# A conditioned two-layer decoder trunk: the residual gates formed as columns on VectorE and spread through DRAM, their PSUM bank given to the transposes

## The chip, the cores and the metric

The kernel runs on one core of one Trainium2 chip. The metric is the device time of one execution in microseconds (us); lower is better. The core's engines are called PE (TensorE: matmuls and transposes), DVE (VectorE), ACT (ScalarE), POOL (GpSimd) and SP (SyncE, which here issues most DMAs). SBUF is the on-chip memory of 128 partitions; PSUM is the memory of eight banks into which PE writes.

## The reference

A sequence of 256 tokens of width 1024 passes two layers. Each layer has three sub-layers: a half-step SwiGLU feed-forward part (FFN, inner width 2816), a token mixer (MoBA attention in layer 0, MLA attention in layer 1, 16 heads each), and a second FFN. All arithmetic is float32. Every sub-layer normalizes its input, shifts and scales it, and adds its result through a gate; shift, scale and gate are vectors of 1024 that a condition vector c gives through one large matrix:

```
c_act = silu(c)
for layer in range(DEPTH):
    mods = c_act @ ada_w[layer] + ada_b[layer]
    sh1, sc1, g1, sh2, sc2, g2, sh3, sc3, g3 = jnp.split(mods, 9, axis=-1)
    h = modulate(rms_norm(x, norm_g[layer, 0]), sh1, sc1)
    x = x + 0.5 * g1[:, None, :] * swiglu(h, ...)
    h = modulate(rms_norm(x, norm_g[layer, 1]), sh2, sc2)
    x = x + g2[:, None, :] * mix
    h = modulate(rms_norm(x, norm_g[layer, 2]), sh3, sc3)
    x = x + 0.5 * g3[:, None, :] * swiglu(h, ...)
```

Layer 1 computes one more pair of shift and scale for its shared keys and values. So there are twenty vectors of 1024: six gates, and fourteen shifts and scales. Each costs a product of c_act with a 1024 x 1024 block of ada_w.

## The kernel before, in words

**Tiles and matmuls.** The 256 tokens lie in two tiles of 128 partitions (t = 0, 1). Each float32 operand of a matmul is split into a high part (hi, gh, h) and a rest (lo, gl), and a product is three matmuls (`mm3`, lines 810 to 812): hi x hi, lo x hi, hi x lo. In the FFN's first half two of the three are merged into one matmul of 512 columns (line 1015), the third has 256 (line 1023). `wload` takes the next weight tile of up to 1 MB from a stream on SP into one of three `raw` buffers (line 787), and `split` (lines 677 to 682) makes hi on ACT (line 680) and lo on DVE (line 681) into a ring of eight each.

**The stages**, with the times of the profile: the first FFN, whose first six blocks `first` computes while the first weights arrive (to about 50 us) and whose rest runs to some 213 us; MoBA to 330; the FFNs of both layers' ends and starts to 700; MLA to 800; the last FFN to the end. During the first FFN a side program builds the bias tables of MoBA. Between two stages stands a norm: `resid` (lines 916 to 931) multiplies the sum by the gate (`ry`, line 920, DVE), adds it to x (line 921) and takes the sum of squares (lines 839 to 842); `rstd_of` (line 847) raises it to the power -0.5 on POOL; ACT scales x to y (line 855), PE transposes it (line 860), ACT or DVE shifts and scales it (lines 876, 878), and the result is split into h (lines 825, 826). In the attentions `head_rstd` (line 1187) has a power on POOL for each group of heads (`hr`).

**The conditioning vectors.** `first` forms the first shift and scale itself; `ada_stream` goes through the other eighteen vectors in eight steps each, paced by PE's work (`ada_pace`). Every step loads one [128, 1024] block of 512 KB (`adaw`, line 707, SP, ring of three).
- Shifts and scales (`column`, line 688): the blocks are transposed on the host. DVE multiplies a block by c_act, which stands in all partitions (`c_b`), and sums along the row; the sum is one column of [128, 8] (line 691: the product and a short read of the accumulator).
- Gates (`ada_gate`, line 721): the blocks are not transposed. POOL clears a [128, 1024] tile `acc` (line 727) and loads the bias into its first row (line 728); DVE adds, eight times, a block times a column of c_act (line 729). Then the column sums of `acc` are wanted in all partitions: `acc` is split into hi and lo, PE multiplies each half by a matrix of ones (lines 739 and 740: four matmuls of 512 columns a gate) into the one bank of the pool `ps_ada`, and ACT copies the bank to the gate's tile with the factor 0.5 or 1 (line 742).

**PSUM.** Eight banks: four for sums (`ps_mm`), three for transposes and scores (`ps_tr`), one for the gates (`ps_ada`, line 588). `first` borrows the gates' bank for its second transpose (line 1624).

**The order.** The program's instructions are put in order by the class `Order`: it lists all with their dependences and buffers, works out when each is due, and places them one by one on the five queues with a table of costs. Then it tries changed due times: each number in `TRIALS` (line 200) is the seed of one random change, and a change is kept where the placed program comes out shorter by those costs. The order found is fixed by dependences, so each engine runs its list in just that order, and a waiting instruction holds up all that stand behind it on its engine.

Of the kernel before, what the change touches and what calls it, by code (L numbers as in the profile page):

```python
# [12 lines left out]
F32 = mybir.dt.float32  # L13
# [9 lines left out]
P = 128  # L23
# [107 lines left out]
def lay_out(v):  # L131

    import numpy as np

    def tiled(w, kt):
        return w.reshape(kt, P, -1).transpose(1, 0, 2).reshape(-1)

    out = {"w": np.concatenate([  # L140
        tiled(np.concatenate([v[n][at][k0 * P:(k0 + kt) * P, c:c + cols] for n, at, c in parts], axis=1), kt)
        for parts, k0, kt, cols in weight_tiles()])}
    out["first"] = np.stack([v["ffn_w_" + n][0, 0, :, :B1 * P].reshape(KD, P, B1, P) for n in ("gate", "up")], axis=3)
    first = out["first"].reshape(KD, P, -1)
    out["first"] = np.concatenate([first[:, :, :FIRST_A].reshape(KD, -1), first[:, :, FIRST_A:].reshape(KD, -1)], axis=1)
    mats, cols, rows = [], np.zeros((P, 3, NK), np.float32), []
    for key, i in vectors():
        w, b, c = ((v["kv_ada_w"], v["kv_ada_b"], i) if key == "kv" else
                   (v["ada_w"][key[0]], v["ada_b"][key[0]], 3 * key[1] + i))
        w, b = w[:, c * D:(c + 1) * D], b[c * D:(c + 1) * D]  # L150
        mats.append((w if i == 2 else w.T).reshape(KD, P, D))
        if i == 2:
            rows.append(b)
        else:
            c0 = NORMS.index(key) * KD
            cols[:, i, c0:c0 + KD] = b.reshape(KD, P).T
    gains = np.concatenate([v["norm_g"].reshape(6 * KD, P), v["kv_norm_g"].reshape(KD, P)])
    cols[:, 2] = gains.T
    pos = np.ascontiguousarray(v["positions"].reshape(S))
    out["c"] = np.concatenate([v["c"].reshape(4, S), np.zeros((28, S), np.float32)])  # L160
    more = [v["c"].reshape(KD, P).T, pos.view(np.float32).reshape(NT, P).T]
    for n in ("moba_q_g", "moba_k_g"):
        more.append(np.tile(v[n][0], 2)[:, None])
    for g in (v["mla_q_g"][0], v["mla_k_g"]):
        more += [np.concatenate([g[:DH], np.ones(P - DH, np.float32)])[:, None], np.tile(g[None, DH:], (P, 1))]
    out.update(ada=np.stack(mats), rows=np.stack(rows), cols=np.concatenate([cols.reshape(P, -1), *more], axis=1))


    table = np.concatenate([np.zeros((1, H), np.float32), v["rel_bias"]])
    keys = pos.view(np.float32).reshape(NT, NB, 4).transpose(0, 2, 1)[:, :, None].repeat(NB, axis=2).reshape(NT, P, NB)  # L170
    end = np.concatenate([table[-1:], np.zeros((NB - 1, H), np.float32)])
    out["tab"] = np.concatenate([*[np.tile(x, (4, 1)) for x in (table[1:], table[:-1], end)], *keys], axis=1)
    for n in ("x", "positions", "kv_a_norm_g", "mla_q_a_norm_g"):
        out[n] = v[n]
    return out


def bcast_row(ap, n, parts=P):
# [18 lines left out]
GATE_MARGIN = 3000.0  # L197
ROUND_OF_ORDER = 4

TRIALS = (23, 24, 58, 84, 106, 187, 193, 252, 302, 317, 381, 394, 424, 459, 553, 591, 607, 655, 706, 722, 891,  # L200
          1035, 1303, 1712, 2361, 2399, 2425, 2605, 2752, 3000, 3292)
ENGINES = ("PE", "DVE", "Activation", "Pool", "SP")


# [370 lines left out]
def trunk(ctx: ExitStack, tc: tile.TileContext, a: dict, out: bass.AP):  # L575
# [8 lines left out]
    sp = ctx.enter_context(tc.tile_pool(name="sp", bufs=8))  # L584
    dp = ctx.enter_context(tc.tile_pool(name="dp", bufs=1, space=DRAM))
    ps_mm = ctx.enter_context(tc.tile_pool(name="ps_mm", bufs=4, space=PSUM))
    ps_tr = ctx.enter_context(tc.tile_pool(name="ps_tr", bufs=3, space=PSUM))
    ps_ada = ctx.enter_context(tc.tile_pool(name="ps_ada", bufs=1, space=PSUM))

    uid = [0]  # L590

    def nm(s):
        uid[0] += 1
        return f"{s}_{uid[0]}"
# [23 lines left out]
    def pe(us):  # L618
        clock[0] += us
        if busy[0]:  # L620
            return
        while pend and pend[0][0] <= clock[0]:
            run_next()
        while pace[0] and clock[0] >= pace[1]:
            pace[1] += pace[0]
            ada(1)
# [23 lines left out]

    ident = cp.tile([P, P], F32, name="ident")
    make_identity(nc, ident)
    ones_r = cp.tile([P, P], F32R, name="ones_r")
    ones = ones_r.bitcast(F32)
    nc.vector.memset(ones, 1.0)
    ident_b = cp.tile([P, P], BF16, name="ident_b")
    nc.vector.tensor_copy(ident_b, ident)
    mhalf = cp.tile([P, 8], F32, name="mhalf")
# [3 lines left out]

    pos_f = a["positions"].rearrange("o s -> (o s)")

    all_cols = cp.tile([P, 3 * NK + KD + NT + 4 + 2 * RO], F32, name="cols")
    places = {}
    c0 = 3 * NK
    for name, n in (("c", KD), ("pos", NT), ("moba_q", 1), ("moba_k", 1), ("q", 1), ("q_pe", RO), ("k", 1), ("k_pe", RO)):
        places[name] = all_cols[:, c0:c0 + n]
        c0 += n  # L670
    cols, cact = all_cols[:, :3 * NK].rearrange("p (i c) -> p i c", i=3), places["c"]
# [16 lines left out]
    def column(key, i, k, wt):  # L688

        c = NORMS.index(key) * KD + k  # L690
        nc.vector.tensor_tensor_reduce(wt, wt, c_b, 1.0, cols[:, i, c:c + 1], op0=ALU.mult, op1=ALU.add,  # L691
                                       accum_out=m_cols[:, i, c:c + 1])

    def scale_col(key, k0=0, n=KD):
        s = col_slice(1, key, k0, n)
# [9 lines left out]
    def ada_tile(j, k):  # L705
        wt = adap.tile([P, D], F32, tag="adaw", name=nm("adaw"))
        nc.sync.dma_start(wt, a["ada"][j, k])
        return wt
# [11 lines left out]

    def ada_gate(j, key, row):

        for k in range(KD):
            with noted(late if key == (1, 2) else set()):
                if k == 0:
                    acc = adap.tile([P, D], F32, tag="acc", name=nm("acc"), bufs=1)
                    nc.gpsimd.memset(acc, 0.0)
                    nc.gpsimd.dma_start(acc[0:1, :], a["rows"][row:row + 1, :])
                nc.vector.scalar_tensor_tensor(acc, ada_tile(j, k), cact[:, k:k + 1], acc, op0=ALU.mult, op1=ALU.add)  # L729
            if k < KD - 1:  # L730
                yield
        ahi, alo = split(acc, D)
        t = mods[key, "g"] = modp.tile([P, D], F32, tag="gate", name=nm("gate"))

        def sums():
            for hh in range(2):
                pt = ps_ada.tile([P, 512], F32, tag="ada", name=nm("adaps"))
                sl = slice(hh * 512, (hh + 1) * 512)
                nc.tensor.matmul(pt, ones_r, ahi[:, sl], start=True, stop=False)
                nc.tensor.matmul(pt, ones_r, alo[:, sl], start=False, stop=True)  # L740
                pe(0.44)
                nc.scalar.activation(t[:, sl], pt, AF.Copy, scale=1.0 if key[1] == 1 else 0.5)
            ready.add((key, "g"))
        later(3.0, sums)
        yield

    def ada_stream():
# [440 lines left out]
        return r  # L1188


    bias_d = dp.tile([3, P // NB, P, H * NB], F32, name="bias_d")


# [371 lines left out]
    def first(units):  # L1565
# [5 lines left out]
        with ExitStack() as st:  # L1571
# [49 lines left out]
                for i in range(2):  # L1621
                    nc.scalar.activation(c_b[:, i * 512:(i + 1) * 512], pc[i], AF.Copy)
            hold(lambda: nc.scalar.activation(cact, cact, AF.Silu), 10e3)
            ps_x = [tr_tile(), ps_ada.tile([P, 512], F32, tag="ada", name=nm("tr"))]
            accs = [tr_tile() if f >= 4 else mm_tile() for f in range(B1)]


# [117 lines left out]
```

## Time and profile before

| | before |
|---|---|
| three timed runs, us | 990.71, 990.8, 993.58 |
| median, us | 990.8 |
| span of the profiled execution, first to last instruction, us | 988.2 |
| median less that span, us | 2.6 |
| TensorE clock granted, mean | 1.000 |

The profiled execution's own time is not recorded beside its span; where a span is carried over to a time, the 2.6 us of the last difference are added. The profile is of one execution. "Busy" counts the time in which an engine executes; matmul records overlap one another, so the cost of a matmul is read from the distance between starts, not from the length of a record. A row of a group gives line, engine, operation, tiles written and read, shapes and count, then busy time in us and the mean of one in ns, then the idle time just before and what ended it. A row of the timeline gives the start, the length, the engine and the line, with the idle time and its releaser in brackets.

### The profile page before, as it was taken

The page shows a single profiled execution, that of the slowest core. Times are in us where ns is not written, and L with a number is a line of the kernel's source. Part 1 is how long each engine was busy: PE and PEld are TensorE (multiplying, and loading weights), DVE is VectorE, ACT ScalarE, POOL GpSimd, SP SyncE. Part 2 cuts the span into 40 slices and gives each one's busy share as a digit, 9 for nine tenths or more (in the row PEclk, how much of TensorE's full clock was granted, in tenths as well). Part 3 has the DMA queues.
Part 4 walks back from the last instruction along what each step waited for, and adds up shares of the span by engine and source line. Part 5 has one row for each costly group of instructions (what it writes and reads, how often), then busy time and mean ns, then how long its engine had stood idle before and what let it go on. Part 6 is the DMA issues. An engine that isn't in the chain of part 4 may idle for free.

```text
span 988.2 us, 15338 instructions
## 1 busy us (share of the span) xinstructions
PE 975.4 (99%) x5580; PEld 832.0 (84%) x5583; DVE 845.5 (86%) x1433; ACT 630.4 (64%) x1180; POOL 82.7 (8%) x120
## 2 busy tenths in 40 slices
PE   8999999999999999999999999999999999999998
PEld 6988888888887788888888888888888888888887
DVE  7999999899998899999889999984899789767642
ACT  6699565378756866656367566553889796657421
POOL 1021010022230100000000000000042110000000
PEclk9999999999999999999999999999999999999999
DMA  9978989898786688888988888883343467544630
GB/s 363 409 262 289 323 305 346 321 344 305 274 322 221 228 289 326 308 299 316 353 325 308 320 325 327 297 320 108 106 158 129 171 229 265 213 188 170 233 130 22
DMA packets 53420, 260.57 MB, mean 264 GB/s; under 512 B 6208, under 2 KB 7008, under 8 KB 35168
## 3 DMA queue, kind: packets, MB, share of 16 engines
q1 hardware_dynamic: 51840, 255.93, 70.7%
q0 software_dynamic: 1024, 3.17, 1.1%
q8 instruction: 44, 0.72, 0.3%
q10 hardware_dynamic: 480, 0.49, 0.2%
q14 instruction: 32, 0.26, 0.1%
HBM read 255.37 MB, written 4.19 MB: 263 GB/s over the span
## 4 chain that ended last, share of the span: by engine, by line
PE 87%; DMA 4%; DVE 4%; issue 2%; ACT 1%; POOL 1%; SPq 0%; ACTq 0%; DVEq 0%; POOLq 0%
PE mm L1015 23%; PE mm L810 15%; PE mm L811 15%; PE mm L812 15%; PE mm L1023 12%; DMA raw<-in_first_dram 3%; PE at L1150 1%; PE at L1090 1%; PE at L1130 1%; DMA bias_d<-bt 1%; DVE lo L681 1%; PE tr L860 1%; DMA raw<-in_w_dram 1%; PE tr L1522 1%; PE at L1095 1%
## 5 line engine op out<-in xcount | busy, mean ns | idle before, releaser
L681 DVE TENSOR_TENSOR lo<-raw,hi 128x1024 fp32r<-128x1024 f32 (+3 forms) x312 | 367.8, 1197 | 69.6 <-ACT hi L680 56.3
L680 ACT ACTIVATE hi<-raw 128x1024 fp32r<-128x1024 f32 (+3 forms) x312 | 316.6, 1037 | 138.9 <-PE mm L812 100.4
L1015 PE MATMUL mm<-h,hi 128*128 128x512 f32 x1120 | 278.9, 392 | 1.0 <-DVE g L955 1.0
L1015 PEld LDWEIGHTS mm<-h,hi 128*128 128x128 f32 x1120 | 202.9, 188 | 38.6 <-DVE g L955 1.4
L1023 PE MATMUL mm<-h,lo 128*128 128x256 f32 x1120 | 157.8, 283 | 0.0
L1023 PEld LDWEIGHTS mm<-h,lo 128*128 128x128 f32 x1120 | 150.4, 191 | 8.8
L691 DVE CUSTOM_DVE_ANT_0 adaw<-adaw,c_b,cols 128x1024 f32<-128x1024 f32 x112 | 141.9, 1278 | 6.6 <-DMA adaw<-in_ada_dram 4.6
L810 PE MATMUL mm<-hi,gh 128*128 128x512 f32 (+1 forms) x356 | 138.0, 388 | 0.0
L811 PE MATMUL mm<-lo,gh 128*128 128x512 f32 (+1 forms) x356 | 137.9, 387 | 0.0
L812 PE MATMUL mm<-hi,gl 128*128 128x512 f32 (+1 forms) x356 | 137.8, 387 | 0.0
L810 PE MATMUL mm<-hi,h 128*128 128x512 f32 (+1 forms) x240 | 93.7, 398 | 0.4 <-ACT h L825 0.4
L811 PE MATMUL mm<-lo,h 128*128 128x512 f32 (+1 forms) x240 | 93.2, 392 | 0.2 <-DVE lo L681 0.2
L812 PE MATMUL mm<-hi,h 128*128 128x512 f32 (+1 forms) x240 | 91.4, 391 | 0.0
L812 PEld LDWEIGHTS mm<-hi,gl 128*128 128x128 f32 x356 | 66.9, 188 | 13.5
L811 PEld LDWEIGHTS mm<-lo,gh 128*128 128x128 f32 x356 | 66.9, 188 | 13.4
L810 PEld LDWEIGHTS mm<-hi,gh 128*128 128x128 f32 x356 | 66.9, 188 | 13.3
L729 DVE SCALAR_TENSOR_TENSOR acc<-adaw,cols,acc 128x1024 f32<-128x1024 f32 x48 | 61.8, 1287 | 0.1
L954 ACT ACTIVATE g<-mm 128x256 f32<-128x256 f32 x70 | 26.4, 377 | 54.8 <-PE mm L1023 51.6
L810 PEld LDWEIGHTS mm<-hi,h 128*128 128x128 f32 x240 | 44.9, 188 | 10.1 <-issue 1.3
L812 PEld LDWEIGHTS mm<-hi,h 128*128 128x128 f32 x240 | 45.0, 188 | 9.0 <-DVE h L826 0.4
L811 PEld LDWEIGHTS mm<-lo,h 128*128 128x128 f32 x240 | 45.1, 188 | 8.4 <-DVE lo L681 0.4
L825 ACT ACTIVATE gh<-g 128x256 fp32r<-128x256 f32 x76 | 31.1, 412 | 30.2 <-DVE g L958 30.1
(241 smaller groups left out, 1224.5 us busy)
## 6 DMA issues: line engine op xcount, KB each, us to landing
raw<-in_w_dram SPq DMA_DIRECT2D x142, 1024.0 KB, 5.5
adaw<-in_ada_dram SPq DMA_DIRECT2D x160, 512.0 KB, 5.5
raw<-in_w_dram SPq DMA_DIRECT2D x12, 512.0 KB, 3.8
raw<-in_first_dram SPq DMA_DIRECT2D x7, 512.0 KB, 9.1
raw<-in_w_dram SPq DMA_DIRECT2D x6, 576.0 KB, 3.8
bias_d<-bt SPq DMA_DIRECT2D x12, 256.0 KB, 4.9
bg<-bias_d POOLq DMA_DIRECT2D x4, 768.0 KB, 6.0
raw<-in_first_dram SPq DMA_DIRECT2D x10, 256.0 KB, 8.4
```

The costliest lines, as they stand in the source:

```text
L680: nc.scalar.activation(hi, src, AF.Copy)
L681: nc.vector.tensor_tensor(lo, src, hi.bitcast(F32), op=ALU.subtract)
L691: nc.vector.tensor_tensor_reduce(wt, wt, c_b, 1.0, cols[:, i, c:c + 1], op0=ALU.mult, op1=ALU.add, accum_out=m_cols[:, i, c:c + 1])
L729: nc.vector.scalar_tensor_tensor(acc, ada_tile(j, k), cact[:, k:k + 1], acc, op0=ALU.mult, op1=ALU.add)
L810: nc.tensor.matmul(ps, lh, rh, start=start, stop=False)
L811: nc.tensor.matmul(ps, lh, rl, start=False, stop=False)
L812: nc.tensor.matmul(ps, ll, rh, start=False, stop=stop)
L825: nc.scalar.activation(hi, ps, AF.Copy)
L860: nc.tensor.transpose(kslice(pt, j), kslice(y, j), ident)
L954: nc.scalar.activation(x, ps[:, S:], AF.Copy)
L1015: nc.tensor.matmul(ps[i], w[0], hs[2], start=k == 0, stop=False)
L1023: nc.tensor.matmul(*low[:3], start=False, stop=low[3])
```

## The change

The six gates are now formed as the shifts and scales are. The host transposes their blocks, with the rows dealt out so that the eight sums of a gate, [128, 8], hold element 8p + k in partition p and column k; their biases come in as 48 more columns of the tile `cols`, which grows from 246 to 294 columns. `column`'s instruction becomes a helper, `dot` (line 692 of the changed kernel), and `ada_gate` calls it eight times with the bias column as the start and as the place of the sum. DVE halves the sums of the four FFN gates (line 730), a POOL DMA stores the 4 KB in a row of a DRAM tile (line 732), and a second POOL DMA, which waits for the first, loads the row into all 128 partitions of the gate's tile (line 733).

So the clearing and the bias load on POOL, the split of `acc`, the four matmuls and the two copies of each gate are gone, and with them the matrix of ones. The bank of `ps_ada` goes to the ring of the transposes, which now has four; `first` takes both of its transposes' banks there. `TRIALS` holds 22 new seeds instead of 31 others, so the order of the whole program is drawn anew. The lines of the changed kernel are counted on their own: line 910 there is 920 before, 850 is 860, 837 is 847, 1177 is 1187, 679 is 681.

```diff
-        mats.append((w if i == 2 else w.T).reshape(KD, P, D))
         if i == 2:
-            rows.append(b)
+            mats.append(w.T.reshape(P, KD, D).transpose(1, 0, 2))
+            gates.append(b.reshape(P, KD))
         else:
+            mats.append(w.T.reshape(KD, P, D))
...
-TRIALS = (23, 24, 58, 84, 106, 187, 193, 252, 302, 317, 381, 394, 424, 459, 553, 591, 607, 655, 706, 722, 891,
...
+TRIALS = (30003, 30017, 30030, 30038, 30042, 30043, 30065, 30073, 30088, 30098, 30112, 30114, 30123, 30124, 30152,
...
-    ps_tr = ctx.enter_context(tc.tile_pool(name="ps_tr", bufs=3, space=PSUM))
-    ps_ada = ctx.enter_context(tc.tile_pool(name="ps_ada", bufs=1, space=PSUM))
+    ps_tr = ctx.enter_context(tc.tile_pool(name="ps_tr", bufs=4, space=PSUM))
...
-    ones_r = cp.tile([P, P], F32R, name="ones_r")
-    ones = ones_r.bitcast(F32)
-    nc.vector.memset(ones, 1.0)
...
-    all_cols = cp.tile([P, 3 * NK + KD + NT + 4 + 2 * RO], F32, name="cols")
+    all_cols = cp.tile([P, 3 * NK + KD + NT + 4 + 2 * RO + 6 * KD], F32, name="cols")
...
-        nc.vector.tensor_tensor_reduce(wt, wt, c_b, 1.0, cols[:, i, c:c + 1], op0=ALU.mult, op1=ALU.add,
-                                       accum_out=m_cols[:, i, c:c + 1])
+        dot(wt, cols[:, i, c:c + 1], m_cols[:, i, c:c + 1])
+
+    def dot(wt, start, col):
+        nc.vector.tensor_tensor_reduce(wt, wt, c_b, 1.0, start, op0=ALU.mult, op1=ALU.add, accum_out=col)
...
+        g = places["gates"][:, row * KD:(row + 1) * KD]
         for k in range(KD):
             with noted(late if key == (1, 2) else set()):
-                if k == 0:
-                    acc = adap.tile([P, D], F32, tag="acc", name=nm("acc"), bufs=1)
-                    nc.gpsimd.memset(acc, 0.0)
-                    nc.gpsimd.dma_start(acc[0:1, :], a["rows"][row:row + 1, :])
-                nc.vector.scalar_tensor_tensor(acc, ada_tile(j, k), cact[:, k:k + 1], acc, op0=ALU.mult, op1=ALU.add)
+                dot(ada_tile(j, k), g[:, k:k + 1], g[:, k:k + 1])
             if k < KD - 1:
                 yield
-        ahi, alo = split(acc, D)
+        if key[1] != 1:
+            nc.vector.tensor_scalar(g, g, 0.5, None, op0=ALU.mult)
         t = mods[key, "g"] = modp.tile([P, D], F32, tag="gate", name=nm("gate"))
-
-        def sums():
-            for hh in range(2):
-                pt = ps_ada.tile([P, 512], F32, tag="ada", name=nm("adaps"))
-                sl = slice(hh * 512, (hh + 1) * 512)
-                nc.tensor.matmul(pt, ones_r, ahi[:, sl], start=True, stop=False)
-                nc.tensor.matmul(pt, ones_r, alo[:, sl], start=False, stop=True)
-                pe(0.44)
-                nc.scalar.activation(t[:, sl], pt, AF.Copy, scale=1.0 if key[1] == 1 else 0.5)
-            ready.add((key, "g"))
-        later(3.0, sums)
+        nc.gpsimd.dma_start(gate_d[row].rearrange("(p k) -> p k", k=KD), g)
+        nc.gpsimd.dma_start(t, bcast_row(gate_d[row], D))
+        ready.add((key, "g"))
         yield
...
-            ps_x = [tr_tile(), ps_ada.tile([P, 512], F32, tag="ada", name=nm("tr"))]
+            ps_x = [tr_tile() for _ in range(2)]
```

Where instructions stand on an engine, before and now, the prediction shows at three places.

More of the change, by code (lines that the diff above doesn't have):

```diff
@@ L145, in lay_out @@
     out["first"] = np.concatenate([first[:, :, :FIRST_A].reshape(KD, -1), first[:, :, FIRST_A:].reshape(KD, -1)], axis=1)
-    mats, cols, rows = [], np.zeros((P, 3, NK), np.float32), []
+    mats, cols, gates = [], np.zeros((P, 3, NK), np.float32), []
     for key, i in vectors():
@@ L165, in lay_out @@
         more += [np.concatenate([g[:DH], np.ones(P - DH, np.float32)])[:, None], np.tile(g[None, DH:], (P, 1))]
-    out.update(ada=np.stack(mats), rows=np.stack(rows), cols=np.concatenate([cols.reshape(P, -1), *more], axis=1))
+    out.update(ada=np.stack(mats), cols=np.concatenate([cols.reshape(P, -1), *more, *gates], axis=1))
     table = np.concatenate([np.zeros((1, H), np.float32), v["rel_bias"]])
@@ L198 @@
 ROUND_OF_ORDER = 4
-TRIALS = (23, 24, 58, 84, 106, 187, 193, 252, 302, 317, 381, 394, 424, 459, 553, 591, 607, 655, 706, 722, 891,
-          1035, 1303, 1712, 2361, 2399, 2425, 2605, 2752, 3000, 3292)
+TRIALS = (30003, 30017, 30030, 30038, 30042, 30043, 30065, 30073, 30088, 30098, 30112, 30114, 30123, 30124, 30152,
+          30165, 30226, 30230, 30319, 30491, 30718, 31097)
 ENGINES = ("PE", "DVE", "Activation", "Pool", "SP")
@@ L663, in trunk @@
     pos_f = a["positions"].rearrange("o s -> (o s)")
-    all_cols = cp.tile([P, 3 * NK + KD + NT + 4 + 2 * RO], F32, name="cols")
+    all_cols = cp.tile([P, 3 * NK + KD + NT + 4 + 2 * RO + 6 * KD], F32, name="cols")
     places = {}
     c0 = 3 * NK
-    for name, n in (("c", KD), ("pos", NT), ("moba_q", 1), ("moba_k", 1), ("q", 1), ("q_pe", RO), ("k", 1), ("k_pe", RO)):
+    for name, n in (("c", KD), ("pos", NT), ("moba_q", 1), ("moba_k", 1), ("q", 1), ("q_pe", RO), ("k", 1), ("k_pe", RO),
+                    ("gates", 6 * KD)):
         places[name] = all_cols[:, c0:c0 + n]
@@ L1188, in head_rstd @@
         return r
+    gate_d = dp.tile([6, D], F32, name="gate_d")
     bias_d = dp.tile([3, P // NB, P, H * NB], F32, name="bias_d")
```

## The prediction, made before the changed kernel was run

> **What bounds the kernel now.** I read the page first, then a table of stretches, then the waits.
>
> ```profile
> span 988.2 us, 15338 instructions
> PE 975.4 (99%) x5580; PEld 832.0 (84%) x5583; DVE 845.5 (86%) x1433; ACT 630.4 (64%) x1180; POOL 82.7 (8%) x120
> PE 87%; DMA 4%; DVE 4%; issue 2%; ACT 1%; POOL 1%; SPq 0%; ACTq 0%; DVEq 0%; POOLq 0%
> ```
>
> TensorE (PE) is busy 975.4 of 988.2 us and carries 87% of the chain that ended last. So PE idles 12.8 us in all. Where, the stretches say (columns: PE, weight loads, DVE, ACT, POOL busy with counts, PE clock, DMA share, GB/s):
>
> ```profile
> 0.00:50.00 50.00, 44.95 (x335) 39.52 (x336) 43.17 (x85) 31.82 (x56) 3.93 (x26) 1.00 0.99 386
> 50.00:100.00 50.00, 50.00 (x522) 44.29 (x522) 48.17 (x117) 45.54 (x98) 8.74 (x40) 1.00 0.77 273
> 100.00:125.00 25.00, 24.02 (x133) 20.65 (x132) 23.31 (x31) 14.25 (x24) 1.62 (x3) 1.00 0.90 322
> 125.00:325.00 200.00, 200.00 (x1064) 164.84 (x1062) 183.25 (x334) 128.31 (x239) 31.57 (x19) 1.00 0.83 302
> 325.00:350.00 25.00, 23.50 (x112) 18.80 (x112) 21.70 (x32) 22.16 (x49) 3.00 (x1) 1.00 0.68 242
> 350.00:700.00 350.00, 350.00 (x1826) 299.94 (x1825) 311.94 (x462) 203.21 (x340) 7.29 (x7) 1.00 0.81 297
> 700.00:800.00 100.00, 98.66 (x635) 85.67 (x637) 91.35 (x213) 85.56 (x212) 25.96 (x24) 1.00 0.41 142
> 800.00:975.00 175.00, 175.00 (x915) 150.29 (x914) 119.01 (x161) 99.53 (x167) 0.57 (x1) 1.00 0.53 197
> ```
>
> PE idles 5.05 us in the first 50 us. From there to 975 us it idles only 0.98 + 1.50 + 1.34 = 3.8 us, and the remaining 4.0 us of the 12.8 lie at the end. The clock stands at 1.00 throughout. So a matmul slot taken out between 125 and 975 us shortens the span by that slot, and no other engine can give more than those 3.8 us back before 975.
>
> **The change part by part.** First PE. Four matmuls a gate, 24 in all, form the column sums and spread them.
>
> ```profile
> L739 PE MATMUL adaps<-hi,ones_r x12: 389/394/397, 121.9 to 898.0; 128*128 128x512 f32 x12
> L740 PE MATMUL adaps<-lo,ones_r x12: 389/394/397, 125.9 to 898.3; 128*128 128x512 f32 x12
> 130.49 0.39 PE L739 MATMUL adaps<-hi,ones_r 128*128 128x512 f32 x1
> 130.72 0.39 PE L740 MATMUL adaps<-lo,ones_r 128*128 128x512 f32 x1
> 130.94 0.64 PE L1023 MATMUL mm<-h,lo 128*128 128x256 f32 x4
> ```
>
> A record is 0.39 us long, but the starts lie 130.94 - 130.49 = 0.45 us apart for two: records overlap, and a slot is 0.225 us. 24 x 0.225 = 5.4 us. All lie from 121.9 us on, where PE idles 3.8 us in 850, so I count all of it as gain. The Trainium skill (TensorE: Matmul & The Clock Gate, Back-to-back issue gap) gives N/2.4 + 2.5 ns for one isolated matmul on a warm array, 216 ns for 512 columns, and 131 ns sustained; by these the term would be 5.2 or 3.1 us, an estimate. The trace's 225 ns sides with the first.
>
> The order of PE at the second half of the first gate, in the first FFN (adaps is the gate's bank, mm the accumulators, hi and lo the split weights), before:
>
> ```order
> L1023 MATMUL mm_1892<-h_108,lo_1822 128x256
> L1015 MATMUL mm_2016<-h_108,hi_1839 128x512
> L1023 MATMUL mm_1891<-h_108,lo_1723 128x256
> L1015 MATMUL mm_2017<-h_108,hi_2020 128x512
> L739 MATMUL adaps_1900<-hi_1856,ones_r 128x512
> L740 MATMUL adaps_1900<-lo_1857,ones_r 128x512
> L1023 MATMUL mm_1892<-h_108,lo_1826 128x256 x4
> L1015 MATMUL mm_2016<-h_108,hi_1843 128x512 x4
> ```
>
> And now, at the same point of PE's work:
>
> ```order
> L1013 MATMUL mm_1883<-h_104,lo_1712 128x256 x4
> L1013 MATMUL mm_1884<-h_104,lo_1815 128x256 x4
> L1005 MATMUL mm_2000<-h_104,hi_1832 128x512 x4
> L1005 MATMUL mm_2000<-h_104,hi_1836 128x512 x4
> L1005 MATMUL mm_2001<-h_104,hi_2004 128x512 x4
> L1013 MATMUL mm_2000<-h_104,lo_1833 128x256 x4
> ```
>
> The two gate matmuls are gone and the FFN's own run in unbroken fours; nothing takes their place.
>
> DVE, ACT and POOL:
>
> ```profile
> L729 DVE SCALAR_TENSOR_TENSOR acc<-adaw,cols,acc 128x1024 f32<-128x1024 f32 x48 | 61.8, 1287 | 0.1
> L691 DVE CUSTOM_DVE_ANT_0 adaw<-adaw,c_b,cols 128x1024 f32<-128x1024 f32 x112 | 141.9, 1278 | 6.6 <-DMA adaw<-in_ada_dram 4.6 <-ACT c_b L1622 2.0
> L691 DVE DVE_READ_ACCUMULATOR2_ANT m_cols<- 128x1 f32 x112 | 9.1, 81 | 0.0
> L681 DVE TENSOR_TENSOR lo<-acc,hi 128x1024 fp32r<-128x1024 f32 x6 | 7.3, 1217 | 2.1 <-PE mm L1023 2.1
> L680 ACT ACTIVATE hi<-acc 128x1024 fp32r<-128x1024 f32 x6 | 6.3, 1056 | 4.5 <-PE mm L812 2.5 <-DVE acc L729 1.7 <-PE mm L1015 0.2
> L742 ACT ACTIVATE gate<-adaps 128x512 f32<-128x512 f32 x12 | 7.1, 592 | 2.6 <-PE adaps L740 2.6
> L727 POOL MEMSET acc<- 128x1024 f32 x6 | 5.7, 955 | 131.7 <-DVE lo L681 131.7
> L1186 DVE TENSOR_SCALAR hv<-hv 128x8 f32<-128x8 f32 x8 | 1.4, 169 | 0.2
> ```
>
> DVE loses 48 x 1.287 + 6 x 1.217 = 69.1 us and gains 48 x (1.278 + 0.081) + 4 x 0.169 = 65.9 us (the column form has rows already, in the shifts and scales): 3.2 us less. ACT loses 6.3 + 7.1 = 13.4 us, POOL 5.7 us of clearing. None of the three ends the span; what their relief is worth lies between 0 and the 3.8 us of idle PE. The fourth bank of the transposes' ring (line 588 before) comes out of the same 3.8 us. In its size this is the unknown of the sum, and the new seeds, which redraw the order, can also take it below nothing. I look at the largest single idle:
>
> ```profile
> 336.63 0.44 PE L860 MATMUL tr<-ident,y 128*128 128x128 f32 x2 [1.37 <-ACT y L855]
> 333.04 3.00 POOL L847 TENSOR_TENSOR rstd<-ssq,mhalf 128x1 f32<-128x1 f32 x1 [8.32 <-DVE ssq L840]
> 328.83 1.28 DVE L729 SCALAR_TENSOR_TENSOR acc<-adaw,cols,acc 128x1024 f32<-128x1024 f32 x1
> 330.02 0.68 DVE L920 TENSOR_TENSOR ry<-mm,gate 128x512 f32<-128x512 f32 x1
> ```
>
> It is the norm after MoBA: the last residual, the sum of squares, POOL's power (3.00 us), then the transposes. A gate product (328.83) stands ahead of the residual. DVE there, before (ry and x the residual, ssq the norm's sum, h the next input, lo a weight split):
>
> ```order
> L826 TENSOR_TENSOR h_3880<-y_3885,h_3880 128x2x128
> L729 SCALAR_TENSOR_TENSOR acc_4022<-adaw_4183,cols,acc_4022 128x1024
> L920 TENSOR_TENSOR ry_3963<-mm_3625,gate_2669 128x512
> L826 TENSOR_TENSOR h_3880<-y_3887,h_3880 128x2x128
> L921 TENSOR_TENSOR x_102<-x_102,ry_3963 128x512
> L840 TENSOR_SCALAR ssq_762_3927<-ssq_762_3927 128x1
> L681 TENSOR_TENSOR lo_4013<-raw_4006,hi_4012 128x1024
> L840 TENSOR_SCALAR ssq_767_3966<-ssq_767_3966,ssq_762_3927 128x1
> ```
>
> And now:
>
> ```order
> L816 TENSOR_TENSOR h_3851<-y_3856,h_3851 128x2x128
> L679 TENSOR_TENSOR lo_3984<-raw_3977,hi_3983 128x1024
> L910 TENSOR_TENSOR ry_3934<-mm_3596,gate_2649 128x512
> L830 TENSOR_SCALAR ssq_750_3898<-ssq_750_3898 128x1
> L911 TENSOR_TENSOR x_97<-x_97,ry_3934 128x512
> L816 TENSOR_TENSOR h_3851<-y_3858,h_3851 128x2x128
> L679 TENSOR_TENSOR lo_4015<-raw_4012,hi_4014 128x1024
> L830 TENSOR_SCALAR ssq_755_3937<-ssq_755_3937,ssq_750_3898 128x1
> ```
>
> A weight split of the same length stands where the product stood, so the chain is about as long; the product has moved behind the sum. I take 0.5 us for all relief together, an eighth of the 3.8, because this place shows so little of it.
>
> Now the new round trip: a store of 128 x 8 (4 KB) to DRAM, then a load of the row into 128 partitions (512 KB), both from POOL.
>
> ```profile
> L728 POOL DMA_DIRECT2D acc<-in_rows_dram x6: 501/547/669, 2.5 to 796.7; - x6
> adaw<-in_ada_dram SPq DMA_DIRECT2D x160, 512.0 KB, 5.5
> DMA to landing us min/median/max: 5.9/6.0/11.6
> 116.53 1.28 DVE L729 SCALAR_TENSOR_TENSOR acc<-adaw,cols,acc 128x1024 f32<-128x1024 f32 x1
> 184.87 0.69 DVE L920 TENSOR_TENSOR ry<-mm,gate 128x512 f32<-128x512 f32 x1
> ```
>
> The third row is POOL's bias load (768 KB). Even two landings as slow as its slowest, 2 x 11.6 = 23 us, fit between the first gate's last product (ends 117.8) and its first use (184.87): 67 us, in which the FFN runs on. In the new order the other gates too stand well over a hundred DVE rows ahead of their use. So the trip costs nothing on the path; without that cover it would be some 11 us a gate (5.5 + 6.0). What stands behind it is POOL's queue, where the load waits for the store. POOL at the start of MoBA (rstd the norm, bg the bias, hr the heads' norm), before:
>
> ```order
> L727 MEMSET acc_4022 128x1024
> L728 DMA acc_4022<-in_rows_dram 1x16x64
> L1304 DMA bg_2808<-bias_d 128x12x128
> L847 TENSOR_TENSOR rstd_2793<-ssq_457_2790,mhalf 128x1
> L1187 TENSOR_TENSOR hr_2870<-hv_482_2869,mhalf 128x8
> L1187 TENSOR_TENSOR hr_2976<-hv_504_2975,mhalf 128x8
> ```
>
> And now:
>
> ```order
> L1295 DMA bg_2779<-bias_d 128x12x128
> L837 TENSOR_TENSOR rstd_2764<-ssq_445_2761,mhalf 128x1
> L732 DMA gate_d<-cols 128x8
> L1177 TENSOR_TENSOR hr_2841<-hv_470_2840,mhalf 128x8
> L733 DMA gate_2649<-gate_d 128x1024
> L1177 TENSOR_TENSOR hr_2947<-hv_492_2946,mhalf 128x8
> ```
>
> The store goes out ahead of the first hr, the waiting load stands ahead of the second.
>
> ```profile
> 218.83 1.53 POOL L847 TENSOR_TENSOR rstd<-ssq,mhalf 128x1 f32<-128x1 f32 x1 [3.91 <-DVE ssq L840]
> 228.42 1.76 POOL L1187 TENSOR_TENSOR hr<-hv,mhalf 128x8 f32<-128x8 f32 x1 [8.06 <-DVE hv L1186]
> 233.27 2.56 POOL L1187 TENSOR_TENSOR hr<-hv,mhalf 128x8 f32<-128x8 f32 x1 [3.09 <-DVE hv L1186]
> ```
>
> Issued near 222, a store that lands in up to 11.6 us is there by 233.6, just as the second hr wants POOL: 0 to about 1 us of delay on POOL, in a stretch where PE is full. I take 0. At this place the Trainium skill speaks against the change (SBUF — State Buffer, Two separate sides: the "DVE blocks DMA" trap): a DMA issued from POOL waits for its descriptors while DVE runs certain instructions; its figures, 620 ns alone against 3100 ns overlapped, would put the second hr some 2.5 us later, an estimate. The trace speaks against it here: POOL's six issues lie within 501 to 669 ns though DVE is busy nine tenths of the time.
>
> The larger column tile (294 against 246 floats in each of 128 partitions) brings 25 KB more into the first stretch, at 386 GB/s 0.06 us: I count 0.1. The clearing of the ones, the host's layout and the first stage's bank (two banks are needed there, before and now) count nothing; PE's 5.05 us of idle at the start covers them.
>
> Sum: 988.2 - 5.4 - 0.5 + 0.1 = 982.4 us of span. The median of the three runs is 990.8, so 2.6 us lie outside the span if that execution was a median one: 985.0 us. About 0.3%, 3 us, is what a measurement of this kernel can tell from no change.
>
> **The rivals.** *The idle goes too.* ACT, DVE and the fourth bank could take most of the 3.8 us: 985.4 - 3.8 = 981.6 at best. For it: DVE at 90%. Against: the norm above. 0.15.
>
> *The new order gives it back.* The seeds are a fresh draw. If PE's idle between 50 and 975 us doubles, the time is 985.4 + 3.8 = 989.2. For it: that idle rests on a few places where one instruction of 1.2 us, put ahead of another, decides. Against: PE's work can mostly be rearranged around it. 0.17.
>
> *The transfers become the bound: slower.* Six loads of 512 KB are 3.1 MB; at the 297 GB/s of 350 to 700 us that is 1.8 us each, 10.6 us in all. If the weights came only just in time, each load would push them back by its length, and the matmul slots saved would only be idle: 990.8 + 10.6 = 1001. It decides from the point where over 8.4 us of it reach PE (5.4 saved plus 3). For it: DMA share 0.8 to 0.9 where five of the gates fall.
>
> ```profile
> SPq L787 <- DVE lo L681: 460.3, 138, 12.9
> ```
>
> Against: SP waits 460 us in all for DVE to free a weight buffer, so transfers wait for buffers, not PE for transfers. 0.05.
>
> *It does not do what it says.* If PE's records hide waits, removed slots would only lengthen them: 990.8. The even 0.225 us spacing speaks against. 0.03.
>
> **How the numbers follow.** The forecast has 0.60, at 985.0. The range drops most of the slower rival and the ends of the first two: 982.2 (985.0 less three quarters of 3.8) to 988.4 (985.0 plus nine tenths). Faster by over 3 us, so under 987.8: 0.60 + 0.15 + 0.03 of the lost order, 0.78. Within: 0.14 + 0.03 = 0.17. Slower: 0.05.
>
> **What would show it.** In the new profile: 24 matmuls fewer and PE busy near 970; 48 more rows of the column form at 1.28 us; PE idle from 50 to 975 us near 3.3 us; the store and load on POOL with landings far ahead of line 910. PE idle over 6.8 us there, or PE's releasers naming the gate or POOL, would make it wrong.

## The result, and the profile after

The changed kernel takes 983.97 us (median of four runs, 983.73 to 984.34), the kernel before 991.56 (four runs, 990.71 to 993.58): a ratio of 0.9927, interval 0.9911 to 0.9944. In the four later calls the kernel before had medians of 990.75 to 991.43. So the gain is 6.8 to 7.6 us, and the time lies 1.0 us under the forecast of 985.0.

The page of the changed kernel, its span, its engines and its chain:

```profile
span 982.6 us, 15317 instructions
...
PE 970.8 (99%) x5556; PEld 829.0 (84%) x5559; DVE 834.4 (85%) x1478; ACT 616.7 (63%) x1162; POOL 85.5 (9%) x120
...
PE 89%; DVE 4%; DMA 4%; ACT 1%; POOL 1%; issue 1%; SPq 0%; POOLq 0%; DVEq 0%; ACTq 0%
```

The span is 5.6 us shorter: PE's busy time has fallen by 4.6 us and its idle time from 12.8 to 11.8 us. The stretches of before, now (PE, weight loads, DVE, ACT, POOL, PE clock, DMA share, GB/s):

```profile
0.00:50.00 50.00, 45.95 (x337) 41.70 (x338) 43.34 (x84) 31.56 (x56) 3.23 (x24) 0.93 0.99 388
50.00:100.00 50.00, 50.00 (x523) 44.56 (x522) 49.18 (x120) 44.98 (x99) 12.17 (x40) 1.00 0.75 264
100.00:125.00 25.00, 25.00 (x142) 21.93 (x141) 25.00 (x43) 15.38 (x27) 2.37 (x4) 1.00 0.99 379
125.00:325.00 200.00, 199.91 (x1065) 164.31 (x1064) 180.17 (x343) 127.18 (x242) 28.21 (x18) 1.00 0.83 302
325.00:350.00 25.00, 25.00 (x120) 20.53 (x119) 24.51 (x40) 20.17 (x40) 2.69 (x3) 1.00 0.85 299
350.00:700.00 350.00, 349.17 (x1831) 299.91 (x1830) 308.88 (x487) 201.49 (x344) 6.96 (x8) 1.00 0.82 300
700.00:800.00 100.00, 97.27 (x611) 82.66 (x613) 87.28 (x203) 83.02 (x207) 28.60 (x22) 1.00 0.43 151
800.00:975.00 175.00, 175.00 (x915) 150.25 (x914) 113.83 (x163) 92.90 (x152) 1.27 (x3) 1.00 0.53 191
```

From 50 to 975 us PE idles 0.09 + 0.83 + 2.73 = 3.65 us, against 3.8 before. The sum has hardly changed, but the places have: the idle at 100 to 125 (0.98) and at 325 to 350 (1.50) is gone, and some has come at 350 to 700 and in MLA. The first stretch shows a clock of 0.93 in this one execution, and matmul records there are longer (L1683 `tr`, 309 ns; 281 before), so its busy time is not to be set against the one before; others of the same kernel, at 1.00, had spans of 982.0. Without these 50 us PE's busy time has fallen from 930.5 to 924.9 us, by 5.6, and its idle time is 7.8 us both times. So in this pair of traces the whole difference of the spans, 5.6 us, is about the length of the 24 slots.

The new work, by groups, the 160 products of the column form among them:

```profile
L692 DVE CUSTOM_DVE_ANT_0 adaw<-adaw,c_b,cols 128x1024 f32<-128x1024 f32 x160 | 203.3, 1284 | 2.5 <-ACT raw L1628 1.6 <-DMA adaw<-in_ada_dram 0.9
...
L692 DVE DVE_READ_ACCUMULATOR2_ANT cols<- 128x1 f32 x48 | 3.9, 82 | 0.0
...
L732 POOL DMA_DIRECT2D gate_d<-cols x6 | 3.7, 610 | 216.3 <-DVE cols L730 143.6 <-DVE cols L692 72.7
L733 POOL DMA_DIRECT2D gate<-gate_d x6 | 3.3, 552 | 19.9 <-DMA gate_d<-cols 17.8 <-issue 2.1
```

There are 48 rows more of the form, at 1.284 us and a read of 0.082 us. POOL stands 17.8 us in all, in four waits, between a store and its load (line 733, the row's last field). Whether somebody waits for that is read at the start of MoBA, the place that the prediction named:

```profile
214.70 1.53 POOL L837 TENSOR_TENSOR rstd<-ssq,mhalf 128x1 f32<-128x1 f32 x1 [2.52 <-DVE ssq L830]
216.19 0.60 POOL L732 DMA_DIRECT2D gate_d<-cols  x1
223.17 1.68 POOL L1177 TENSOR_TENSOR hr<-hv,mhalf 128x8 f32<-128x8 f32 x1 [6.38 <-DVE hv L1176]
224.81 0.59 POOL L733 DMA_DIRECT2D gate<-gate_d  x1
230.17 2.57 POOL L1177 TENSOR_TENSOR hr<-hv,mhalf 128x8 f32<-128x8 f32 x1 [4.77 <-DVE hv L1176]
```

Nobody does here: the load goes out at 224.81, and POOL then idles 4.77 us until DVE has the values of the second hr. For the other five loads the trace lists no waiter either. The landings of the stores (line 732), then of the loads (line 733):

```profile
DMA to landing us min/median/max: 2.2/4.7/7.7
...
DMA to landing us min/median/max: 5.4/6.7/9.8
```

And the first use of a gate on DVE:

```profile
179.00 0.68 DVE L910 TENSOR_TENSOR ry<-mm,gate 128x512 f32<-128x512 f32 x1
```

The first load is issued at 123.3 us and its gate is used at 179.0: over 45 us to spare even with the longest landing.

### The profile page after: what moved, and what is told of

Read it like the earlier page. It is cut to its first block, busy times and chain, and to the rows that moved or that the text cites. A ratio compares the mean times of both kernels' runs of the same rounds, so it can differ in the third digit from the quotient of the medians.

```text
span 982.6 us, 15317 instructions
## 1 busy us (share of the span) xinstructions
PE 970.8 (99%) x5556; PEld 829.0 (84%) x5559; DVE 834.4 (85%) x1478; ACT 616.7 (63%) x1162; POOL 85.5 (9%) x120
## 4 chain that ended last, share of the span: by engine, by line
PE 89%; DVE 4%; DMA 4%; ACT 1%; POOL 1%; issue 1%; SPq 0%; POOLq 0%; DVEq 0%; ACTq 0%
PE mm L1005 26%; PE mm L800 14%; PE mm L801 14%; PE mm L802 14%; PE mm L1013 14%; DMA raw<-in_first_dram 4%; PE at L1140 1%; PE tr L850 1%; PE tr L1242 1%; PE at L1120 1%; DVE lo L679 1%; POOL hr L1177 1%; PE at L1085 1%; PE tr L1513 0%; DVE mx L1094 0%
## 5 line engine op out<-in xcount | busy, mean ns | idle before, releaser
L1005 PE MATMUL mm<-h,hi 128*128 128x512 f32 x1120 | 268.1, 391 | 0.0
L1005 PEld LDWEIGHTS mm<-h,hi 128*128 128x128 f32 x1120 | 205.7, 188 | 39.7
L692 DVE CUSTOM_DVE_ANT_0 adaw<-adaw,c_b,cols 128x1024 f32<-128x1024 f32 x160 | 203.3, 1284 | 2.5 <-ACT raw L1628 1.6
L1013 PEld LDWEIGHTS mm<-h,lo 128*128 128x128 f32 x1120 | 144.4, 191 | 5.5
L1013 PE MATMUL mm<-h,lo 128*128 128x256 f32 x1120 | 148.3, 284 | 0.0
L1177 POOL TENSOR_TENSOR hr<-hv,mhalf 128x4 f32<-128x4 f32 (+1 forms) x24 | 41.0, 1708 | 63.1 <-DVE hv L1176 53.9
```

Source lines behind the costliest of these rows:

```text
L692: nc.vector.tensor_tensor_reduce(wt, wt, c_b, 1.0, start, op0=ALU.mult, op1=ALU.add, accum_out=col)
L1005: nc.tensor.matmul(ps[i], w[0], hs[2], start=k == 0, stop=False)
L1013: nc.tensor.matmul(*low[:3], start=False, stop=low[3])
L1177: nc.gpsimd.tensor_tensor(r, v2, mhalf[:, :nh], op=ALU.pow)
```

## The experiments

The theory: the gain is the 24 slots of PE, and the rest of the change is small. Against it stood the seeds (a luckier order), the bank, the relief of DVE and ACT, and the transfers. Twelve kernels were timed, in five rounds each. "Over before" is the ratio to the kernel before on the same chip in the same rounds.

| kernel | median us | over before, interval | span us | PE busy us |
|---|---|---|---|---|
| before, new seeds | 992.99 | 1.0012 [0.9998, 1.0026] | 991.3 | 978.1 |
| before, no seeds | 993.25 | 1.0019 [1.0009, 1.0029] | 991.0 | 977.2 |
| changed, old seeds | 984.08 | 0.9923 [0.9909, 0.9937] | 982.3 | 971.0 |
| changed, no seeds | 985.97 | 0.9943 [0.993, 0.9957] | 984.1 | 971.7 |
| changed, 24 spare matmuls | 991.31 | 1.0002 [0.9992, 1.0012] | 989.5 | 977.3 |
| changed, spare passes on ACT and DVE | 985.68 | 0.9943 [0.9926, 0.9961] | 983.7 | 970.9 |
| changed, own bank back | 986.16 | 0.9948 [0.993, 0.9965] | 984.0 | 972.0 |
| changed, each row loaded thrice | 985.38 | 0.994 [0.9921, 0.9959] | 983.4 | 970.6 |
| changed, no seeds, old tail as spare work | 991.01 | 0.9996 [0.9984, 1.0008] | 989.3 | 977.3 |
| the same, in an own bank | 994.80 | 1.0038 [1.0024, 1.0052] | 992.9 | 978.8 |
| the same, with ACT's copies too | 994.30 | 1.0033 [1.002, 1.0046] | 992.3 | 979.9 |
| before, no seeds, matmuls asked for later | 993.94 | 1.0033 [1.0021, 1.0045] | 992.6 | 978.4 |

**The change and the seeds, crossed.** Four kernels: each of the two with the other's seeds, and each with none (the edit of the last two, the list shortened).

```diff
-TRIALS = (23, 24, 58, 84, 106, 187, ...
+TRIALS = ()
```

> The kernel before with the 22 new seeds, nothing else. Theory of the slots (the gain is 24 matmul slots of 0.225 us, 5.4 us, whatever the order): this stays at the time before, 989 to 992 us, PE busy near 975.4. Rival, the draw of the order: the gain is the seeds', and this comes near the time after, 984 to 986.

> The changed kernel with the 31 old seeds. Theory of the slots: PE busy near 970.8 as after, and the time 984 to 987, some 5.4 us under the kernel before, since PE's idle between 50 and 975 us was 3.8 us in both orders. Rival, the draw of the order: back to 988 to 991, with PE idle there over 7 us.

> The kernel before with no seeds at all, so its order is the one that is placed first. It tells what seeds are worth here. Both theories leave its level open; my estimate is 0.5 to 1.5% above before, 996 to 1006 us, with the difference in PE's idle and not in PE's busy time (975.4).

> The changed kernel with no seeds at all. Theory of the slots: 5.4 us under the kernel before without seeds, give or take 2 us for the other idle of another order; PE busy 4.6 to 5.4 us less. Rival, the draw of the order: no difference between the two without seeds, or one over 10 us of either sign.

The change is worth 993.25 - 985.97 = 7.3 us without seeds and 991.43 - 984.08 = 7.35 with the old ones (991.43 is before in those rounds). The changed kernel is as fast with the old seeds (984.08) as with its own (983.97). Seeds are worth 1.8 us before (993.25 to 991.43) and 2.0 after (985.97 to 983.97), much less than I had estimated; the new seeds, put on the kernel before, do nothing (992.99 against 993.25, and 1 us over the 992 expected), but `Order` keeps only one of the 22 there, so this pair says little. The pair without seeds says it: the draw isn't the gain. But 7.3 is 2 us more than the 5.4 of the slots. All three orders of before have one wait in common, which no order of the changed kernel has. Without seeds, the stretch of 100 to 125 us in the kernel before and then PE's row there, and the same stretch in the changed kernel:

```profile
100.00:125.00 25.00, 23.90 (x133) 20.54 (x132) 24.56 (x34) 13.92 (x25) 3.01 (x4) 1.00 0.96 363
```

```profile
119.29 1.21 PE L1014 MATMUL mm<-h,hi 128*128 128x512 f32 x4 [1.10 <-DVE g L954]
```

```profile
100.00:125.00 25.00, 25.00 (x142) 21.94 (x141) 25.00 (x44) 15.03 (x28) 2.26 (x5) 1.00 0.98 355
```

PE waits 1.10 us for DVE's product g, which empties an accumulator. It happens at the end of the first gate. The next two groups of kernels ask what in the old gate's tail (split, matmuls, bank, copies) brings it.

**Slots, passes, bank and loads, one each.** First the slots alone:

```diff
...
+        def spare():
+            for _ in range(2):
+                pt = tr_tile()
+                for i in range(2):
+                    nc.tensor.matmul(pt, ones_r, wide_r, start=i == 0, stop=i == 1)
+                pe(0.44)
+        later(3.0, spare)
```

> The changed kernel with the 24 matmuls of 512 columns back as spare work: four behind each gate's sums, of a matrix of ones with itself, into a bank of the transposes' ring that nobody reads. Theory of the slots (now: 24 slots of 0.225 us are 5.4 us of the gain, and the other 2 us are DVE's and ACT's relief at the first gate, where PE waited 1.0 to 1.1 us near 119 us for DVE's product in all three orders of the kernel before): after plus 5.4, so 989 to 990, with no PE idle between 100 and 125 us. Rival, that slots are only part of it and PE's records hide waits: under 987. Rival, that the matmuls themselves made the other 2 us: 991 or more.

Then the passes of the split, the bank, and two more loads a gate:

```diff
...
+        nc.scalar.activation(wt, wt, AF.Copy)
+        nc.vector.tensor_tensor(wt, wt, c_b, op=ALU.subtract)
```

> The changed kernel with one pass of 1024 columns on ACT and one on DVE added behind each gate's eight sums, in place on the last block, whose content is no longer used: the length of the old split of the gate's sum, 6 x (1.06 + 1.22) us, without its matmuls. Theory of relief: the wait near 119 us comes back, PE idle of some 1 us between 100 and 125 us, and the time is 1 to 2 us over after, 985 to 986. Rival, that DVE and ACT have room: 984.0 plus or minus 0.5 and no idle there.

```diff
-    ps_tr = ctx.enter_context(tc.tile_pool(name="ps_tr", bufs=4, space=PSUM))
+    ps_tr = ctx.enter_context(tc.tile_pool(name="ps_tr", bufs=3, space=PSUM))
+    ps_ada = ctx.enter_context(tc.tile_pool(name="ps_ada", bufs=1, space=PSUM))
...
```

> The changed kernel with the fourth bank taken from the transposes' ring again: three, and one that is used once, by the first stage's second transpose. Theory of the slots: the bank gives at most 1 us, 984.0 to 985.0. Rival, the bank gave the 2 us over the 5.4 (the norm after MoBA, where PE idled 1.37 us before and not after): 985.5 to 987, with idle of PE between 325 and 350 us over 0.5 us.

```diff
-        nc.gpsimd.dma_start(t, bcast_row(gate_d[row], D))
+        for _ in range(3):
+            nc.gpsimd.dma_start(t, bcast_row(gate_d[row], D))
```

> The changed kernel with every gate's row loaded three times into the gate's tile: 12 loads more of 512 KB, 6.3 MB, from POOL. Theory: the load is hidden, transfers wait for buffers; 984.0 to 984.7, and POOL's two extra issues a gate (0.55 us each) cost nothing. Rival, transfers bound the middle: 12 x 1.8 = 21 us more, 1000 to 1006, or some 3 us for each extra 2 MB if they bound it only in part.

By these expectations, which start from the changed kernel at 984, all four times miss the theory's side: 991.31 is the rival's "991 or more", 986.16 lies in the range of the bank's rival, 985.68 in that of relief, 985.38 over 984.7. But the idle of PE by which relief and bank were to show is missing: 100 to 125 us is full (25.00 of 25) with the passes, and so is 325 to 350 us with the bank.

The base is in doubt, which I saw only afterwards. The 22 seeds were found for the changed program. `Order`, worked out again from the kernels' files, keeps all 22 there, but in these four, in the order of the table, only 5, 6, 3 and 6. So the nearer base is the changed kernel without seeds, 985.97. It is not an exact one: of the old seeds, too, the changed kernel keeps only 3, and it takes 984.08 with them. So a result of this group alone is known to about 2 us. Against 985.97 the passes (985.68), the bank (986.16) and the loads (985.38) are worth nothing that can be measured (ratios of 0.9943, 0.9948 and 0.994 against 0.9943); against 983.97 they would cost 1.4 to 2.2 us each. The bound by transfers, 21 us, is excluded by either. The DMA table with three loads of each gate, and the two stretches in which most of them fall:

```profile
DMA packets 56010, 270.01 MB, mean 275 GB/s; under 512 B 6496, under 2 KB 7296, under 8 KB 37760
...
gate<-gate_d POOLq DMA_DIRECT2D x18, 512.0 KB, 7.6
```

```profile
125.00:325.00 200.00, 199.42 (x1062) 164.33 (x1061) 180.92 (x343) 126.56 (x242) 29.56 (x21) 1.00 0.85 313
350.00:700.00 350.00, 349.37 (x1834) 300.56 (x1833) 308.21 (x486) 202.34 (x341) 9.92 (x14) 1.00 0.83 308
```

6.3 MB more are moved, the rate rises to 313 GB/s, and PE is as full as before. The 21 us of the rival are not there.

The spare matmuls cost 991.31 - 985.97 = 5.3 us by the kernel without seeds, 7.3 by the changed kernel itself. Their group and the stretch of 100 to 125 us in that kernel:

```profile
L744 PE MATMUL tr<-ones_r x24: 387/393/397, 122.3 to 895.7; 128*128 128x512 f32 x24
```

```profile
100.00:125.00 25.00, 25.00 (x141) 21.94 (x140) 25.00 (x44) 14.87 (x28) 3.02 (x4) 1.00 0.98 359
```

With the matmuls back, there is still no wait of PE near 119 us, so the matmuls alone don't bring it. What they cost, a pair without seeds has to tell.

**The old tail, put back in steps.** To the changed kernel without seeds: the split and the 24 matmuls of its halves; then the own bank; then ACT's copies. None of it is used. Then, from the other side, the kernel before with its matmuls asked for later.

```diff
...
+        whi, wlo = split(wt, D)
...
+        def spare():
+            for hh in range(2):
+                pt = tr_tile()
+                sl = slice(hh * 512, (hh + 1) * 512)
+                nc.tensor.matmul(pt, ones_r, whi[:, sl], start=True, stop=False)
+                nc.tensor.matmul(pt, ones_r, wlo[:, sl], start=False, stop=True)
+                pe(0.44)
+        later(3.0, spare)
```

> The changed kernel without seeds, with the tail of the old gate back behind the eight column sums as work whose result is not used: a split of the last block in the ring of the weights' splits (1.06 us on ACT, 1.22 on DVE, six times), and four matmuls of its halves with a matrix of ones, 24 in all. It lacks only the old products by rows, the gates' own bank and ACT's copies. Base: the changed kernel without seeds, 986.0. Theory of the slots alone: 24 x 0.232 = 5.6 us, so 991.5, no PE idle between 100 and 125 us. Theory that the split, which the matmuls make due early, is what puts DVE's product late near 119 us: another 1.3 to 1.5 us, 992.9, with PE idle of 1 us there. The kernel before without seeds took 993.25.

```diff
...
-                pt = tr_tile()
+                pt = ps_ada.tile([P, 512], F32, tag="ada", name=nm("adaps"))
```

> The kernel of the run before (the changed kernel without seeds, with the old tail, split and 24 matmuls, as unused work), and the gates' own bank back: three banks for the transposes and one in which the 24 matmuls write. What is still missing of the old gate are ACT's copies and the products by rows. That kernel took 991.0, the kernel before without seeds 993.25, so some 2 us are to be placed. Theory of the bank: two halves of a gate take turns in one bank, and the transposes have one less; 992.5 or more. Rival, the bank matters as little here as alone (it took 986.16 against 985.97 without seeds): 991.0 to 991.5.

```diff
+                nc.scalar.activation(junk_b, pt, AF.Copy)
```

> The same with ACT's 12 copies of the bank too (0.59 us each, into a tile that nobody reads). Now only the products by rows, POOL's clearing, the bias row and the way into the gate's tile differ from the kernel before. Theory of the tail: with it all back the time is that of the kernel before without seeds, 993.25 plus or minus 0.5, and PE idles 1 us near 119 us. Rival, that the rest comes with the order that the row form happens to get: 991 to 992, with no idle there.

```diff
-        later(3.0, sums)
+        later(20.0, sums)
```

> The kernel before without seeds, with each gate's four matmuls asked for 20 us of PE's work after the split and not 3. Nothing is left out; the order is drawn from other due times. In the new order one gate product of 1.28 us fewer stands ahead of DVE's g product for which PE waits near 119 us. Theory that the wait there is a matter of DVE's order at the end of the first gate: it shrinks or goes, and the time falls by up to 1.4 us from 993.25, to 991.9. Rival, that the wait comes with the row form itself whatever the order: it stays at 1.0 to 1.1 us of idle, 993 plus or minus 0.5.

Split and matmuls in the ring of four cost 991.01 - 985.97 = 5.0 us, both kernels without seeds: the slots, and the theory that the split brings the wait falls, since 100 to 125 us is full (25.00). The own bank then costs 994.80 - 991.01 = 3.8 us more (by the ratios 0.0042, 4.2 us), though the same bank without matmuls cost 0.2 to 2.2. The copies add nothing (-0.5); 993.25 and a wait near 119 us were expected, and neither came. Both kernels with the own bank lie 1.0 to 1.6 us over the kernel before without seeds, so orders of nearly the same work differ by that much here. PE at the first gate, in the ring of four and then in the own bank (tr and adaps are the banks):

```profile
122.23 0.39 PE L737 MATMUL tr<-hi,ones_r 128*128 128x512 f32 x1
122.46 0.40 PE L738 MATMUL tr<-lo,ones_r 128*128 128x512 f32 x1
122.69 0.40 PE L737 MATMUL tr<-hi,ones_r 128*128 128x512 f32 x1
122.92 0.40 PE L738 MATMUL tr<-lo,ones_r 128*128 128x512 f32 x1
```

```profile
117.89 0.73 PE L1018 MATMUL mm<-h,hi 128*128 128x512 f32 x2 [1.01 <-DVE g L958]
...
119.52 0.40 PE L738 MATMUL adaps<-hi,ones_r 128*128 128x512 f32 x1
...
123.80 0.40 PE L739 MATMUL adaps<-lo,ones_r 128*128 128x512 f32 x1
...
127.34 0.40 PE L738 MATMUL adaps<-hi,ones_r 128*128 128x512 f32 x1
127.58 0.39 PE L739 MATMUL adaps<-lo,ones_r 128*128 128x512 f32 x1
```

In the ring the four run in a row, 0.23 us each. In the own bank they lie spread over 8 us between the FFN's matmuls, as they do in the kernel before, and the wait for g is back, at the same place and with the same releaser.

But the bank isn't all that differs. `Order` has a rule of its own for matmuls into tiles whose name begins with `adaps` (lines 435 and 468 of the kernel before; it still stands in the changed one): it holds each back until it has been ready for 3 us and then puts it ahead of all else on PE. The kernels with an own bank for the gates' matmuls have tiles of that name, the others have none. So this step put back the bank and the rule together. The spreading is the rule's: worked out from the same kernel with the tile under another name, `Order` places the first gate's four matmuls within 1.4 us. What each of the two costs was not measured.

DVE just ahead of that wait, in the kernel with the own bank:

```profile
116.21 1.28 DVE L694 CUSTOM_DVE_ANT_0 adaw<-adaw,c_b,cols 128x1024 f32<-128x1024 f32 x1
...
117.41 0.42 DVE L958 TENSOR_TENSOR g<-mm,g 128x256 f32<-128x256 f32 x1
```

A product of the gate stands ahead of g; PE goes on at 117.89. In the kernel before it is a weight split, with another short product behind it:

```profile
117.73 1.22 DVE L681 TENSOR_TENSOR lo<-raw,hi 128x1024 fp32r<-128x1024 f32 x1
...
119.20 0.41 DVE L955 TENSOR_TENSOR g<-mm,g 128x256 f32<-128x256 f32 x1
```

A long instruction ahead of g isn't enough, though. In the kernel with the ring a g follows a weight split too and starts at 117.75, no earlier than the 117.41 above, while PE runs sixteen matmuls without a wait:

```profile
115.96 3.82 PE L1017 MATMUL mm<-h,hi 128*128 128x512 f32 x16
```

So it is the order of PE and DVE together that makes the wait. The kernel with the copies and the one with later matmuls don't have this wait, but another of the same size at another place. One row of each, the first with the copies:

```profile
54.11 1.43 PE L1020 MATMUL mm<-h,hi 128*128 128x512 f32 x5 [1.31 <-ACT hi L681]
```

```profile
54.29 1.43 PE L1014 MATMUL mm<-h,hi 128*128 128x512 f32 x5 [1.25 <-ACT hi L679]
```

So the expectation for the later matmuls was half right: the wait near 119 is a matter of order and can be drawn away, but the order that has it drawn away pays at 54 us, and the time rose to 993.94 where 991.9 was expected. Six kernels have gate matmuls in a bank of their own (and under `Order`'s rule), and each has one wait of 1.0 to 1.3 us between 50 and 125 us. The eight others, with the matmuls in the ring or with none, idle 0.00 to 0.02 us there.

What stays open is how the bank or the rule does it. PE doesn't wait there for the spread matmuls themselves: in all six kernels the wait is over before the first of them starts (119.29 and 120.34 in the kernel before without seeds, 117.89 and 119.52 with the own bank, 54 and 119 in the two others). What differs is the order that was fixed beforehand for the whole program. And the wait is not the whole step: of the 3.6 us by which the spans of ring and own bank differ, 1.5 are PE's busy time (977.3 and 978.8) with the same 5583 matmuls, 1.0 is this wait, and the rest is other idle, most of it in MoBA and MLA. Why the busy time grows is not known.

No kernel here beats the changed one; with the old seeds it comes out the same.

## Why the prediction was right, point by point

**PE's 24 slots, 5.4 us: right.** Put back in the kernel without seeds, the matmuls cost 5.0 us together with their split; the spare ones cost 5.3 against that kernel. PE's busy time came out at 970.8 for the 970 forecast, and outside the first 50 us it fell by 5.6. The slot is 0.23 us in the rows above, 5.5 us for 24. The Trainium skill (TensorE: Matmul & The Clock Gate, Back-to-back issue gap) has 216 ns and 131 ns; by the second, an estimate, the gain would have been 3.1 us, and the runs exclude that.

**The relief, 0.5 us: mis-sized, and not what I took it for.** This term makes the miss of 1.0. The forecast is the median of before, 990.8, less 5.8 us in all; the measured gain is 6.8 from that median and 7.6 from the median of four, while the slots gave 5.0 to 5.6. So some 1.5 to 2 us stand where I put 0.5. DVE's and ACT's relief as such is not it: the split put back together with the matmuls costs no more than the slots, and the copies add nothing. The 2 us come where the gates' matmuls leave a bank of their own and `Order`'s rule for it, and 1.0 to 1.3 of them can be seen as one wait; bank and rule are not separated, and the order moves other idle as well. In the two traces of before and after this wait and the idle behind MoBA are gone, but nearly as much has come elsewhere (3.8 and 3.65 us), so the cause of these 2 us is shown in part only. The wait's idle stood in the table that I quoted (24.02 of 25 at 100 to 125 us). I looked at the largest single idle, behind MoBA, instead, and at what stands ahead of it on DVE; that chain, which I took to be about as long as before, leaves PE without idle now (25.00 of 25). I had costed the bank within that half microsecond as a ring that is one deeper.

**PE's idle from 50 to 975 us, 3.3: 3.65.** The wait near 119 us is gone and the norm after MoBA runs without idle, and 350 to 700 us (0.83) and MLA (2.73 for 1.34) gave back most of both in this order.

**The 2.6 us outside the span: wrong, but without effect on the forecast.** In the profiled executions of all thirteen kernels since, the time less the span is 1.7 to 2.1 us. By that the profile of before, with 988.2, is of an execution of about 990.0, shorter than its median; that execution's own time isn't recorded. The forecast of the time doesn't hang on it, since 988.2 + 2.6 is the median again. But the span came out near the forecast (982.0 to 982.6 for 982.4) by luck: it was taken from a span about 0.8 us short of the median's, and the gain was taken about 1 us too small. It also means that the pair of profiles, 988.2 to 982.6, shows only 5.6 of the 7 us by which the medians differ.

**The round trip and POOL's queue, 0: right.** The landings of at most 7.7 and 9.8 us lie far ahead of the use, and the load stood ahead of no one who could have gone earlier. The rule of the Trainium skill that I had weighed against the change (SBUF — State Buffer, Two separate sides: the "DVE blocks DMA" trap) isn't seen. The store at the first gate is issued in the stretch in which DVE is busy 25.00 of 25.00 us:

```profile
L732 POOL DMA_DIRECT2D gate_d<-cols x1 | 0.7, 722 | 19.0 <-DVE cols L730 19.0
```

It took 722 ns of POOL, the longest of the six, and not 3100. The figures of the Trainium skill are for a whole DMA, though, and not for its issue, as I had read them. The page of the profile has the loads of 512 KB, from POOL and from SP, with their median landing:

```profile
adaw<-in_ada_dram SPq DMA_DIRECT2D x160, 512.0 KB, 6.2
...
gate<-gate_d POOLq DMA_DIRECT2D x6, 512.0 KB, 6.7
```

They differ by 0.5 us.

**The larger cols tile, 0.1: not seen.** PE's idle in the first 50 us went from 5.05 to 4.05 us at the clock of 0.93; with the old seeds, at 1.00, it is 3.95.

**The rivals.** The new order gave nothing back: three orders put the changed kernel at 984.0, 984.1 and 986.0. The idle did not go too. Transfers bound nothing, even with 6.3 MB more. The records did not hide waits in place of slots, since slots put back cost about their length.

## What to carry to other kernels

Where PE is full, count a matmul by the distance between starts: here 24 of 0.23 us cost 5.0 us when they were put back. A bank reserved for small side work, with the rule that the order has for it, can cost more through the order than through its own size: try it together with its user, since alone it cost 0.2 to 2.2 us and with the matmuls and the rule 3.8. An edited program doesn't keep the seeds found for another: compare edits without seeds. And set a span against the time of its own execution before adding what lies around it.

## What the runs showed that I had not expected

The executions of one kernel spread very differently: before from 988.73 to 994.94 us in seventeen runs on one chip, the changed kernel with spare matmuls, of the same length, from 991.07 to 991.51 in twelve there. What varies in the kernel before was not looked into. And 12 more broadcasts of 512 KB from POOL lengthen the median landing only from 6.7 to 7.6 us.
